# Merge gates in the tail: two more token quarters of four chunks in seven half-size products, with half of the sums of x on GpSimd

## The chip, the cores and the metric

The kernel runs on one core of a Trainium2 chip. A time is the device time of one execution in microseconds (us). A profile of one execution shows, for every instruction, when it started and how long it took on each engine: PE (TensorE, matrix products), DVE (VectorE), ACT (ScalarE), POOL (GpSimd) and SP (the queue that issues most DMAs). L1442 is line 1442 of the kernel; the change adds 5 lines ahead of almost everything and more further on, so the same statement has another number in the kernel after.

## The reference, cut to what matters

One layer of a hybrid attention block: `x` is 2048 tokens by 1024 channels, float32.

```python
h = rms_norm(x, norm_gain[layer])
proj = h @ w_in[layer]
qa, ka, va, qb, kb, vb, ga, gb, mg = jnp.split(proj, split_idx, axis=-1)
...                                     # two attention mixers give ya and yb
br_a = ya @ w_branch_a[layer]
br_b = yb @ w_branch_b[layer]
gates = jax.nn.sigmoid(mg.reshape(bsz, S, N_BRANCHES, D) + b_merge[layer])
merged = gates[:, :, 0] * br_a + gates[:, :, 1] * br_b
x = x + merged @ w_out[layer]
```

The change touches the product that gives `mg`, the merge-gate logits: 1024 channels of `h` times 2048 columns (1024 for each of the two branches), for 2048 tokens.

## The kernel before, in words

**Numbers.** Every float32 operand of a product is split into two float16 parts, a high one and a low one, and a product is the sum of three float16 products (high·high, high·low, low·high). The normalized `x`, transposed, lies in SBUF as `XH` and `XL` (128 partitions, 8 channel chunks, 2048 tokens and 256 tokens repeated).

**Stages.** A first stage loads and turns `x`; a long main loop projects and does both attentions; a tail follows. The tail has three stages: the merge gates, the branch products, the output product. The merge gates are cut by columns into chunks of 2 x 128 (one 128 for each branch), and by tokens into four quarters of 512. The first chunk is done in the main loop. The five others are numbered n = 0 to 4 here, in the order of use.

**Two ways for one chunk.** `gate_pair(n, q)` does one quarter plainly: 2 branches x 8 channel chunks x 3 = 48 matmuls of 128x512. `gate_group(n)` does quarters 0 and 2 together with Strassen's scheme in Winograd's form. The weights make a 2x2 of blocks (4 channel chunks by one branch), `x` another (4 channel chunks by one quarter); seven products of 12 matmuls take the place of eight. For that it needs sums: of the weight blocks (T1, T2, T3, N4; `w_sums`) and of the blocks of `x` (S1 to S4; `x_sums`). A sum of `x` is made in float32 from high plus low (the function `whole`), then split again: ACT rounds the high part (`hi`), DVE makes the low part (`lo`). The sums of `x` are the same for all chunks. In the kernel before, DVE makes all of them, in four groups c = 0 to 3 of one channel chunk each, into places of the buffer `wt` that is needed only later.

**Preparation of a chunk's weights** (`prep`): SP loads them into the one raw buffer `wraw` (four DMAs), POOL multiplies by the norm gains (four operations, L194), ACT squares and adds up (four, L236), PE adds across partitions in one small matmul (`norm_sum`, L211, whose input is `wsq`), DVE works out a power of two as scale, ACT and DVE split (L253, L259), and `w_sums` overwrites `wraw` with the sums of blocks (L1484) and splits these (L1485, L1481). The next chunk's load waits until `wraw` has been read for the last time.

**Output weights.** The last stage also uses seven-product groups; `b_load` and `b_blocks` bring in and split column parts j = 0 to 3 of `w_out` and their sums (L1340, L1341, L1362), in the gate stage.

**What sets the order.** The kernel is recorded with a list of events: `at(t, f)` puts a function at a planned time, and matmuls move the plan's clock (2.6 us for each 12). The tables `T_P`, `T_O`, `T_S` and so on hold such times. Only the order that comes out matters on the chip: each engine takes its instructions strictly in that order and waits where an input isn't there. So a late POOL operation holds up everything behind it on POOL, and a matmul that waits holds up every matmul behind it. In the plan before, PE does quarters 1 and 3 of n = 0 plainly, two of the seven products of n = 0, quarters 1 and 3 of n = 1, and so on: five groups of seven and ten plain quarters.

PSUM gives the tail eight banks of 128x512 (`bank`), used in turn.

Of the kernel before, what the change touches and what calls it, by code (L numbers as in the profile page):

```python
# [32 lines left out]
S = 2048  # L33
# [71 lines left out]
T_G = (143.4, 174.8, 176.0, 177.4)  # L105
T_S = (2.0, 11.0, 0.85, 1.6, 0.75, 1.5, 0.9, 1.3, 0.8)
# [18 lines left out]
def block_kernel(tc, x, w_units, w_gate, w_mrg, w_brn, w_out, w_bra, gain, qkg, sink, bias_a, bias_b, b_merge, out):  # L125
# [1073 lines left out]
    t = 0  # L1199
# [98 lines left out]

    rho, invb = {}, []
    bnd = ucol()  # L1300
    for k, (s, inv) in enumerate(((sa, ia), (sb, ib))):
        mi = ucol()
        V.tensor_tensor(mi[:], yi[4 * k][:], yi[4 * k + 1][:], OP.max)
# [11 lines left out]
    V.tensor_tensor(bnd[:], invb[0][:], invb[1][:], OP.add)
    V.tensor_scalar(bnd[:], bnd[:], 2.0 ** 31, None, OP.mult)
    s_m, i_m = pow2(bnd[:], "m")

    inv_m, rmx = ucol(), ucol()
    V.tensor_tensor(inv_m[:], invb[0][:], invb[1][:], OP.max)  # L1320
    V.reciprocal(rmx[:], inv_m[:])
    for c in range(8):
        V.tensor_scalar(rho[c][:], rho[c][:], invb[c // 4][:], rmx[:], OP.mult, OP.mult)
    V.tensor_scalar(inv_m[:], inv_m[:], s_m[:], 0.125, OP.mult, OP.mult)
    i_o, so4 = ucol(), ucol()
    V.tensor_scalar(i_o[:], i_m[:], io[:], 16.0, OP.mult, OP.mult)
    V.tensor_scalar(so4[:], so[:], 0.25, None, OP.mult)

# [64 lines left out]
    def gate_pair(n, q):  # L1393
        dc, u = DCS[n + 1], NU + 1 + n
        if n not in ims:
            assert ("w", u) in done
            ims[n] = ucol()
            V.tensor_scalar(ims[n][:], wtiles[u][2][:], 0.5 / SX, None, OP.mult)
        for k in range(2):
            ps = bank()  # L1400
            g = fg.tile([128, 512], F32, name="fg", bufs=6)
# [22 lines left out]

    def xsum(i, c):
        m = 4 * i + c
        return [wt[k][:, m % 7, 1 + m // 7, :] for k in range(2)]

    def xblock(b, c):
        if b in sidx:  # L1430
            assert ("xs", sidx[b], c) in done
            return xsum(sidx[b], c)
        o = 1024 if b == A22 else 0
        return [X[:, c + (0 if b == A11 else 4), o:o + 512] for X in (XH, XL)]

    def x_sums(t, c):

        tmp = y0.tile([128, 4, 512], F32, name=f"Y0{c % 2}")
        v1, v2, v3, v4 = (tmp[:, i, :] for i in range(4))

        def whole(o, ch, tok):
            V.tensor_tensor(o, XH[:, ch, tok:tok + 512], XL[:, ch, tok:tok + 512], OP.add)  # L1442

        def hi(v, i):
            A.activation(xsum(i, c)[0], v, AF.Copy, scale=0.25)

        def lo(v, i):
            h, l = xsum(i, c)
            V.scalar_tensor_tensor(l, v, 0.25, h, OP.mult, OP.subtract)
            done.add(("xs", i, c))  # L1450

        steps = ((whole, v1, c, 1024), (whole, v2, c + 4, 1024), (V.tensor_tensor, v2, v1, v2, OP.add), (hi, v2, 0),
                 (whole, v3, c, 0), (V.tensor_tensor, v1, v3, v1, OP.subtract), (lo, v2, 0), (hi, v1, 2),
                 (V.tensor_tensor, v3, v2, v3, OP.subtract), (hi, v3, 1), (whole, v4, c + 4, 0), (lo, v1, 2),
                 (V.tensor_tensor, v4, v4, v3, OP.subtract), (hi, v4, 3), (lo, v3, 1), (lo, v4, 3))
        for k, (f, *args) in enumerate(steps):
            at(t + T_S[2] * k, f, *args)

    tw = {}

    def w_sums(t, n):

        u = NU + 1 + n

        def begin():
            raw, s, inv, wh, wl = wtiles[u]
            q4 = ucol()
            V.tensor_scalar(q4[:], s[:], 0.25, None, OP.mult)
            t2 = [yq.tile([128, 512], F32, name="yq")[:].bitcast(F16).rearrange("p (b c d) -> p b c d", b=2, c=4) for _ in range(2)]
            b11, b12, b21, b22 = (raw[:, 4 * i:4 * i + 4, 128 * j:128 * j + 128] for i in range(2) for j in range(2))  # L1470
# [5 lines left out]
            for k, (b, o, x, y) in enumerate(((T1, o1, b12, b11), (T3, o3, b22, b12), (T2, o2, b22, o1), (N4, o4, b21, o2))):  # L1476
# [6 lines left out]

                at(now[0] + (T_S[3] if n else .72) * k, lambda o=o, x=x, y=y: V.tensor_tensor(o, x, y, OP.subtract))  # L1484
                at(now[0] + T_S[3] * k + T_S[4], lambda h=h, o=o, q4=q4: A.activation(h, o, AF.Copy, scale=q4[:]))  # L1485
# [3 lines left out]

    def gate_group(n):  # L1490
        dc, u = DCS[n + 1], NU + 1 + n
# [20 lines left out]
        def products(ps, x, bl):  # L1512
            mm = []
            for ch in range(4):
                for k, w in ((0, 0), (1, 0), (0, 1)):
                    i = len(mm)
                    mm.append(lambda ch=ch, k=k, w=w, i=i: T.matmul(  # L1517
                        ps[:], lhsT=weight(bl, ch)[w], rhs=xblock(x, ch)[k], start=(i == 0), stop=(i == 11)))
            return mm

        def copy(o, ps, scale):
            A.activation(o, whole(ps), AF.Copy, scale=scale)

        def plus(o, ps, v, scale):
            V.scalar_tensor_tensor(o, whole(ps), scale, v, OP.mult, OP.add)

# [3 lines left out]
        def gate(o, v, k, q, late):  # L1530
            at(now[0] + late, lambda: A.activation(o, v, AF.Tanh, bias=bmh[:, 8 * k + dc:8 * k + dc + 1], scale=ims[n][:]))
            at(now[0] + late + T_S[6], lambda: nc.sync.dma_start(out=whole(mgd[2 * dc + k][:, 512 * q:512 * q + 512]), in_=o))

# [10 lines left out]
        for k, (x, bl, f) in enumerate(steps):  # L1544
            if k == 0 and n:
                a = tile_()
# [5 lines left out]

    t = clock[0]
    for n, b, d in T_P:
        w_sums(t + d, n)
        if n:
            prep(t + b, NU + 1 + n)
    for c in range(4):
        at(t + T_S[0] + T_S[1] * c, x_sums, t + T_S[0] + T_S[1] * c, c)
    for j, b, d in T_O:  # L1560
# [18 lines left out]
    y_part(t + T_G[3], 0, 2, 0.9)  # L1579
    group0 = gate_group(0)  # L1580
    for n, q in ((0, 1), (0, 3), (group0, 2), (1, 1), (1, 3), (group0, 5), (gate_group(1), 7), (2, 1), (2, 3),
                 (gate_group(2), 7), (gate_group(3), 7), (gate_group(4), 7), (3, 1), (3, 3), (4, 1), (4, 3)):
        if isinstance(n, int):
            gate_pair(n, q)
        else:
            for _ in range(q):
                next(n)
    until(clock[0] + T_GATE[4] + .1)
    f1.close()
# [265 lines left out]
```

## Time and profile before

| what | value |
|---|---|
| median of 3 runs | 1910.09 us (1909.49 to 1910.53) |
| the profiled execution: span of its instructions | 1907.4 us |
| how the two stand | the median lies 2.7 us above the span |
| PE busy | 1898.5 us of the span |
| DVE, ACT, POOL busy | 1355.2, 1119.2, 848.7 us |
| gate stage of the tail | from 1399 us to 1593 us |
| branch stage | 1593 to 1759 us |
| output stage | 1759 us to the end |

In a timeline each row gives start, duration, engine, line, operation, output<-inputs, shape and count; a bracket gives the idle time of the engine before it and what ended it. In a table by stretches, each engine has its busy time and, in brackets, the number of its instructions. Names of tiles leave out buffer numbers: `wt` is the buffer of the sums of `x` and later of `w_out`, `fg` a gate tile, `Y` a temporary of 128x512, `yq` a small pool that also holds T2 and N4, `fps` and `pj` PSUM banks, `ubuf` a table of single columns (scales).

### The profile page before, as it was taken

The page shows a single profiled execution, that of the slowest core. Times are in us where ns is not written, and L with a number is a line of the kernel's source. Part 1 is how long each engine was busy: PE and PEld are TensorE (multiplying, and loading weights), DVE is VectorE, ACT ScalarE, POOL GpSimd, SP SyncE. Part 2 cuts the span into 40 slices and gives each one's busy share as a digit, 9 for nine tenths or more (in the row PEclk, how much of TensorE's full clock was granted, in tenths as well). Part 3 has the DMA queues.
Part 4 walks back from the last instruction along what each step waited for, and adds up shares of the span by engine and source line. Part 5 has one row for each costly group of instructions (what it writes and reads, how often), then busy time and mean ns, then how long its engine had stood idle before and what let it go on. Part 6 is the DMA issues. An engine that isn't in the chain of part 4 may idle for free.

```text
span 1907.4 us, 39286 instructions
## 1 busy us (share of the span) xinstructions
PE 1898.5 (100%) x13578; PEld 1190.9 (62%) x13578; DVE 1355.2 (71%) x3522; ACT 1119.2 (59%) x2496; POOL 848.7 (44%) x1848
## 2 busy tenths in 40 slices
PE   8999999999999999999999999999999999999999
PEld 6566776677766688566787667876544444444444
DVE  7578887887767877577776877868686667867312
ACT  8468776777666776566776767666444645423100
POOL 4334454344545655446555666555412211223443
PEclk9999999999999999999999999999999999999999
DMA  8459987798868697578768788666822246887853
GB/s 292 122 106 182 195 171 149 150 195 157 189 108 195 132 186 135 123 149 183 165 128 156 159 181 145 131 125 124 189 73 100 105 155 221 236 253 246 282 209 137
DMA packets 624585, 316.56 MB, mean 166 GB/s; under 512 B 492928, under 2 KB 562176, under 8 KB 623104
## 3 DMA queue, kind: packets, MB, share of 16 engines
q1 hardware_dynamic: 605952, 305.39, 69.3%
q10 hardware_dynamic: 18432, 8.66, 1.8%
q8 instruction: 106, 1.74, 0.4%
q14 instruction: 95, 0.78, 0.1%
HBM read 129.91 MB, written 65.27 MB: 102 GB/s over the span
## 4 chain that ended last, share of the span: by engine, by line
PE 95%; DVE 2%; POOL 1%; issue 1%; ACT 1%; DMA 0%; SPq 0%; DVEq 0%; POOLq 0%; ACTq 0%
PE pj L710 44%; PE pj L334 16%; PE fps L334 11%; PE fps L1722 6%; PE s L880 5%; PE pv L929 5%; PE fps L1517 3%; PE pj L1722 2%; PE pj L610 2%; PE pj L1517 1%; ACT jk L482 0%; DMA xt<-in_x_dram 0%; PE pt L1001 0%; DVE XL L531 0%; DVE pr L895 0%
## 5 line engine op out<-in xcount | busy, mean ns | idle before, releaser
L710 PE MATMUL pj<-wh,XL 128*128 128x384 f16 x1792 | 586.1, 327 | 0.0
L710 PE MATMUL pj<-wl,XH 128*128 128x384 f16 x1792 | 584.7, 326 | 0.0
L710 PE MATMUL pj<-wh,XH 128*128 128x384 f16 x1792 | 584.4, 326 | 0.2 <-DVE vt L742 0.2
L710 PEld LDWEIGHTS <-XH 128*128 128x128 f16 x3584 | 410.4, 116 | 151.0 <-issue 0.9
L895 DVE CUSTOM_DVE_ANT_0 pr<-s,b,ubuf 128x256 f32<-128x256 f32 (+3 forms) x512 | 219.0, 465 | 77.3 <-PE s L880 75.3
L710 PEld LDWEIGHTS <-XL 128*128 128x128 f16 x1792 | 207.8, 116 | 69.1
L912 DVE SCALAR_TENSOR_TENSOR p<-pr,p 128x512 f16<-128x512 f32 (+2 forms) x256 | 190.2, 743 | 19.1 <-ACT p L908 19.0
L787 POOL COPY spl<-spl 128x256 f16<-128x256 f16 (+1 forms) x224 | 88.6, 425 | 183.3 <-DVE spl L782 181.9
L727 ACT ACTIVATE rw<-pj 128x256 f32<-128x256 f32 (+1 forms) x224 | 86.8, 387 | 134.4 <-PE pj L710 123.2
L908 ACT ACTIVATE p<-pr 128x512 f16<-128x512 f32 (+2 forms) x256 | 159.2, 622 | 6.4 <-issue 0.3
L334 PEld LDWEIGHTS <-wh 128*128 128x128 f16 x960 | 93.7, 98 | 110.5
L880 PE MATMUL s<-kq 128*128 128x256 f16 (+3 forms) x1168 | 147.8, 254 | 0.3 <-DMA kq<-spl 0.3
L929 PEld LDWEIGHTS <-pt 128*128 128x128 f16 x3024 | 125.4, 97 | 34.8
L287 POOL TENSOR_TENSOR rs_t<-rs_y 128x8 f32<-128x8 f32 (+1 forms) x112 | 41.2, 368 | 231.3 <-DVE rs_y L279 182.7
L772 POOL TENSOR_TENSOR rw<-rw,g 128x256 f32<-128x256 f32 (+1 forms) x112 | 91.4, 816 | 109.5 <-DVE rw L766 73.1
L194 POOL TENSOR_TENSOR wraw<-wraw,gn 128x768 f32<-128x768 f32 (+1 forms) x80 | 112.5, 1412 | 56.0 <-DMA wraw<-in_w_mrg_dram 43.5
L929 PE MATMUL pv<-vt,pt 128*128 128x65 f16 (+1 forms) x3024 | 132.7, 192 | 0.0
L880 PEld LDWEIGHTS <-kq 128*128 128x128 f16 x1184 | 101.7, 98 | 42.3 <-DMA kq<-spl 0.8
L766 DVE TENSOR_TENSOR rw<-rw,qr 128x512 f32<-128x512 f32 (+1 forms) x112 | 102.6, 916 | 32.0 <-POOL qr L296 31.1
L742 DVE SCALAR_TENSOR_TENSOR vt<-pj,vt 128x128 f16<-128x128 f32 (+1 forms) x224 | 62.1, 277 | 88.6 <-ACT vt L736 87.9
L334 PE MATMUL pj<-XH,gh 128*128 128x512 f16 x320 | 121.3, 379 | 0.0
L334 PE MATMUL pj<-XH,gl 128*128 128x512 f16 x320 | 121.2, 379 | 0.0
(281 smaller groups left out, 3797.9 us busy)
## 6 DMA issues: line engine op xcount, KB each, us to landing
wraw<-in_w_units_dram SPq DMA_DIRECT2D x56, 384.0 KB, 4.4
mtd<-mm SPq DMA_DIRECT2D x56, 256.0 KB, 3.7
M<-mtd SPq DMA_DIRECT2D x8, 1792.0 KB, 9.8
mgd<-fg SPq DMA_DIRECT2D x39, 256.0 KB, 2.1
zd<-z ACTq DMA_DIRECT2D x128, 66.0 KB, 2.5
zz<-zd SPq DMA_DIRECT2D x64, 132.0 KB, 2.8
xt<-in_x_dram SPq DMA_DIRECT2D x16, 512.0 KB, 9.3
gtd<-yo SPq DMA_DIRECT2D x32, 256.0 KB, 2.9
```

The costliest lines, as they stand in the source:

```text
L194: G.tensor_tensor(v, v, gn[:, c0:c0 + 2].unsqueeze(2).to_broadcast([128, 2, n]), OP.mult)
L334: out.append(lambda w=w, xx=xx, ch=ch, i=i: T.matmul(ps[:], lhsT=w[:, ch, c0:c0 + 128], rhs=xx[:, ch, ts], start=(i == 0), stop=(i == n - 1)))
L710: out.append(lambda lhs=lhs, rhs=rhs, ch=ch, k=k: T.matmul(ps[:, :384], lhsT=lhs[:, ch, :], rhs=rhs[:, ch, :], start=(k == 0), stop=(k == ...
L766: V.tensor_tensor(q, q, self.rr[:, :n].unsqueeze(2).to_broadcast([128, n, HD]), OP.mult)
L772: G.tensor_tensor(k, k, GT[un.br][:].unsqueeze(1).unsqueeze(1).to_broadcast([128, 2, un.nk, HD]), OP.mult)
L787: G.tensor_copy(sp[:, i, nh:, :, :], sp[:, i, nq:nh, ::-1, :])
L880: T.matmul(self.sv[j][:, o:o + k1 - k0], lhsT=q[:, h, qo:qo + 128], rhs=kt[:, un.nq + kh + v * un.nk, k0:k1], start=(v == 0), stop=(v == 1))
L895: V.tensor_tensor_reduce(out=self.pv[:, j, self.p0:self.p0 + W], in0=self.sv[j], in1=un.bias[:, self.h0 + j, self.b0:self.b0 + W], scale=I ...
L908: A.activation(self.sp[:, :128 * n], self.pr, AF.Copy, scale=PSC)
L912: V.scalar_tensor_tensor(self.sp[:, 128 * n:], self.pr, PSC, self.sp[:, :128 * n], OP.mult, OP.subtract)
L929: T.matmul(self.po[:, j, :w], lhsT=p[:, n * j + s, :], rhs=un.v[key][:, vh, c0:c0 + w], start=(k == 0 and s == 0), stop=(k == 2 and s == n ...
L1722: mm.append(lambda ch=ch, k=k, w=w, i=i: T.matmul(ps[:, :cols.stop - cols.start], lhsT=m[:, a, ch, k, :], rhs=wt[w][:, b, ch, cols], start ...
```

## The change

Chunks n = 1 to 4 get a second group of seven products for quarters 1 and 3; chunk 0 keeps its two plain quarters. The sums of `x` are made a second time, for quarters 1 and 3 (called p = 1; S1 and S2 go to a new buffer `sx`, S3 and S4 over the part of `XH` and `XL` that has been used up). For c = 2 and 3 POOL makes the additions (`whole` and the others); `lo` stays on DVE, `hi` on ACT. The weight sums of n = 1 to 4 move from DVE to POOL too. T2 and N4 of n = 3 and 4 go to the repeated tokens of `XH` and `XL`. The scales for the later stages, worked out at the start of the tail in one run, become a generator that is stepped through at planned times from 60 us on. Part j = 3 of the output weights moves from the end of the gate stage into the branch stage. `prep` gets a shift that puts `norm_sum` and what follows later by 6.0, 7.0, 5.5 and 1.0 us for n = 1 to 4. A reserved scratch for DMA descriptors is set smaller; it is memory only.

```diff
-T_P = ((0, 0.0, 0.03), (1, 3.0, 50.0), (2, 56.0, 75.0), (3, 82.0, 102.0), (4, 108.5, 128.3))
-T_O = ((0, 62.0, 84.0), (1, 136.4, 154.0), (2, 136.9, 164.6), (3, 183.9, 190.0))
+T_P = ((0, 0.0, 0.03, 0.0), (1, 3.0, 30.6, 6.0), (2, 39.6, 67.4, 7.0), (3, 73.0, 99.5, 5.5), (4, 105.6, 127.5, 1.0))
+T_O = ((0, 62.0, 88.0), (1, 134.4, 147.2), (2, 134.9, 155.4))
+T_OB = (58.0, 66.0)
+T_X = {(0, 0): (0.6, 0.85), (0, 1): (10.2, 0.85), (0, 2): (0.3, 1.35), (0, 3): (11.9, 1.35),
+       (1, 0): (23.0, 0.95), (1, 1): (33.0, 1.1), (1, 2): (24.0, 1.8), (1, 3): (39.5, 1.9)}
...
+    sx = fin.enter_context(tc.tile_pool(name="sx", bufs=1)).tile([128, 8, 2, 512], F16, name="sx")
...
-    def x_sums(t, c):
-
-        tmp = y0.tile([128, 4, 512], F32, name=f"Y0{c % 2}")
-        v1, v2, v3, v4 = (tmp[:, i, :] for i in range(4))
+    def x_sums(t, c, p, d):
+        E = V if c < 2 else G
+
+        if c < 2:
+            tmp = y0.tile([128, 4, 512], F32, name=f"Y0{c}")
+            v1, v2, v3, v4 = (tmp[:, i, :] for i in range(4))
+        else:
+            v1, v2, v3, v4 = (wt[k][:, 5 + i, 2 - i:4 - i, :].rearrange("p a b -> p (a b)").bitcast(F32)
+                              for k in range(2) for i in range(2))
...
-            V.tensor_tensor(o, XH[:, ch, tok:tok + 512], XL[:, ch, tok:tok + 512], OP.add)
+            tok += 512 * p
+            E.tensor_tensor(o, XH[:, ch, tok:tok + 512], XL[:, ch, tok:tok + 512], OP.add)
...
-                at(now[0] + (T_S[3] if n else .72) * k, lambda o=o, x=x, y=y: V.tensor_tensor(o, x, y, OP.subtract))
+                at(now[0] + (T_S[3] if n else .72) * k, lambda o=o, x=x, y=y: (G if n else V).tensor_tensor(o, x, y, OP.subtract))
...
-    for n, q in ((0, 1), (0, 3), (group0, 2), (1, 1), (1, 3), (group0, 5), (gate_group(1), 7), (2, 1), (2, 3),
-                 (gate_group(2), 7), (gate_group(3), 7), (gate_group(4), 7), (3, 1), (3, 3), (4, 1), (4, 3)):
+    for q in (1, 3):
+        gate_pair(0, q)
+    for n, p in ((0, 0), (1, 0), (1, 1), (2, 0), (2, 1), (3, 0), (4, 0), (3, 1), (4, 1)):
+        for _ in gate_group(n, p):
+            pass
...
+    at(t + T_OB[0], b_load, 3)
+    at(t + T_OB[1], b_blocks, t + T_OB[1], 3)
```

How the order of instructions changes, at three places. First POOL at the start of the tail, before; the last operations of the main loop (`zz`), then the gains of chunks n = 1 and 2 (`wraw`) and the additions of the gate groups (L1528).

```order
L1112 TENSOR_TENSOR zz<-zz,bm_e 128x4x64 x3
L194 TENSOR_TENSOR wraw<-wraw,gn 128x2x256 x4
L1528 TENSOR_TENSOR wt_21862<-fg 128x2x256
L1528 TENSOR_TENSOR fg<-fg 128x512
L194 TENSOR_TENSOR wraw<-wraw,gn 128x2x256 x4
```

POOL at the same place in the kernel after, up to the gains of n = 1; `wt_21866` and `wt_21867` are the two halves of `wt`, here the temporaries of c = 2.

```order
L1117 TENSOR_TENSOR zz<-zz,bm_e 128x4x64 x3
L1466 TENSOR_TENSOR wt_21866<-XH,XL 128x512 x2
L439 TENSOR_TENSOR wt_21866<-wt_21866 128x512
L1466 TENSOR_TENSOR wt_21867<-XH,XL 128x512
L439 TENSOR_TENSOR wt_21866<-wt_21867,wt_21866 128x512
L439 TENSOR_TENSOR wt_21867<-wt_21866,wt_21867 128x512
L1466 TENSOR_TENSOR wt_21867<-XH,XL 128x512
L199 TENSOR_TENSOR wraw<-wraw,gn 128x2x256 x2
L439 TENSOR_TENSOR wt_21867<-wt_21867 128x512
L199 TENSOR_TENSOR wraw<-wraw,gn 128x2x256 x2
```

The sums of c = 2 now stand ahead of and between the gains of n = 1, those of c = 3 behind them. Further on in the same queue, the gains of n = 2 among the sums of c = 3 for p = 1:

```order
L439 TENSOR_TENSOR wt_21866<-wt_21866 128x512
L199 TENSOR_TENSOR wraw<-wraw,gn 128x2x256
L1466 TENSOR_TENSOR wt_21867<-XH,XL 128x512
L199 TENSOR_TENSOR wraw<-wraw,gn 128x2x256
L439 TENSOR_TENSOR wt_21866<-wt_21867,wt_21866 128x512
L199 TENSOR_TENSOR wraw<-wraw,gn 128x2x256 x2
L439 TENSOR_TENSOR wt_21867<-wt_21866,wt_21867 128x512
```

From the first sum to the last of these gains stand 43 POOL operations: 8 gains and 35 of two full operands (sums, weight sums, two additions of a gate group). In the kernel before 10 stood there.

Second, PE in the kernel after, where the small matmul of n = 2 (`norm_sum`, L216) now is: in the group of n = 1, p = 1, right ahead of its product with S1 (`sx`); 288 matmuls of 128x512 stand ahead of it in the gate stage.

```order
L1547 MATMUL fps<-XL,wh 128x512
L1547 LDWEIGHTS wl
L1547 MATMUL fps<-XH,wl 128x512
L216 LDWEIGHTS ones
L216 MATMUL pj<-wsq,ones 128x4
L1547 LDWEIGHTS wh
L1547 MATMUL fps<-sx,wh 128x512
```

Before, it stood behind 331 matmuls, and DVE, not POOL, had made all sums. Third, DVE at the start of the tail in the kernel after (`Y_21886` holds weight sums of n = 0, `Y_21891` the sums of c = 0); before, 40 operations on single columns (the scales, L1303 to L1327) stood between the first row here and the second.

```order
L231 RECIPROCAL ubuf<-ubuf 128x1
L1412 TENSOR_SCALAR ubuf<-ubuf 128x1
L1499 TENSOR_SCALAR ubuf<-ubuf 128x1
L1519 TENSOR_TENSOR Y_21886<-wraw 128x512
L1466 TENSOR_TENSOR Y_21891<-XH,XL 128x512
L1519 TENSOR_TENSOR Y_21886<-wraw 128x512
```

DVE begins its sums that much sooner, and makes 80 operations with two SBUF operands (64 for the sums of `x`, 12 for weight sums, 4 for the split of n = 1) up to the last low part of the sums for p = 1.

More of the change, by code (lines that the diff above doesn't have):

```diff
@@ L1315, in block_kernel @@
[L1315 to L1325, printed above, removed]
@@ L1326, in block_kernel, with tail_scales, tt @@
-    V.tensor_scalar(i_o[:], i_m[:], io[:], 16.0, OP.mult, OP.mult)
-    V.tensor_scalar(so4[:], so[:], 0.25, None, OP.mult)
+    rho, invb = [ucol() for _ in range(8)], []
+    bnd, inv_m, rmx, i_o, so4 = (ucol() for _ in range(5))
+    def tail_scales():
+        def tt(*a):
+            V.tensor_tensor(*(v[:] for v in a[:-1]), a[-1])
+        V.tensor_scalar(so4[:], so[:], 0.25, None, OP.mult)
+        for k, (s, inv) in enumerate(((sa, ia), (sb, ib))):
+            mi, rm, iv = ucol(), ucol(), ucol()
+            for c in range(3):
+                tt(mi, mi if c else yi[4 * k], yi[4 * k + c + 1], OP.max)
+                yield
+            V.reciprocal(rm[:], mi[:])
+            yield
+            tt(rm, rm, s, OP.mult)
+            tt(iv, mi, inv, OP.mult)
+            yield
+            for c in range(4 * k, 4 * k + 4):
+                tt(rho[c], rm, yi[c], OP.mult)
+            invb.append(iv)
+        tt(bnd, invb[0], invb[1], OP.add)
+        tt(inv_m, invb[0], invb[1], OP.max)
+        yield
+        V.tensor_scalar(bnd[:], bnd[:], 2.0 ** 31, None, OP.mult)
+        V.reciprocal(rmx[:], inv_m[:])
+        yield
+        s_m, i_m = pow2(bnd[:], "m")
+        for c in range(8):
+            V.tensor_scalar(rho[c][:], rho[c][:], invb[c // 4][:], rmx[:], OP.mult, OP.mult)
+        V.tensor_scalar(inv_m[:], inv_m[:], s_m[:], 0.125, OP.mult, OP.mult)
+        V.tensor_scalar(i_o[:], i_m[:], io[:], 16.0, OP.mult, OP.mult)
@@ L1334, in block_kernel, with run @@
+    def run(steps):
+        if next(steps, run) is not run:
+            at(now[0] + T_R[1], run, steps)
     A11, A12, A22, S1, S2, S3, S4 = range(7)
@@ L1400, in gate_pair @@
             ps = bank()
[L1401 removed]
+            g = fg.tile([128, 512], F32, name="fg", bufs=7)
             def tanh(ps=ps, g=g, k=k):
@@ L1418, in prep, with xsum, xblock @@
         chain(sq)
     sidx = {S1: 0, S2: 1, S3: 2, S4: 3}
[L1425 to L1429, printed above, removed]
+    def xsum(p, i, c):
+        if p == 0:
+            m = 4 * i + c
+            return [wt[k][:, m // 3, 1 + m % 3, :] for k in range(2)]
+        if i < 2:
+            return [sx[:, 4 * i + c, k, :] for k in range(2)]
+        return [X[:, c, 512 * i:512 * i + 512] for X in (XH, XL)]
+    def xblock(b, c, p):
@@ L1465, in begin @@
         def begin():
+            assert ("w", u) in done, (n, now[0] - t0)
             raw, s, inv, wh, wl = wtiles[u]
@@ L1531, in gate @@
             at(now[0] + late, lambda: A.activation(o, v, AF.Tanh, bias=bmh[:, 8 * k + dc:8 * k + dc + 1], scale=ims[n][:]))
-            at(now[0] + late + T_S[6], lambda: nc.sync.dma_start(out=whole(mgd[2 * dc + k][:, 512 * q:512 * q + 512]), in_=o))
+            at(now[0] + late + T_S[6], lambda: nc.sync.dma_start(out=mgd[2 * dc + k][:, 512 * (q + p):512 * (q + p) + 512], in_=o))
         def two(ps):
@@ L1544, in gate_group @@
         for k, (x, bl, f) in enumerate(steps):
-            if k == 0 and n:
+            if k == 0:
                 a = tile_()
@@ L1551, in gate_group @@
             yield
-    t = clock[0]
-    for n, b, d in T_P:
+    t = t0 = clock[0]
+    at(t + T_R[0], run, tail_scales())
+    for n, b, d, late in T_P:
         w_sums(t + d, n)
         if n:
-            prep(t + b, NU + 1 + n)
+            prep(t + b, NU + 1 + n, late)
     for c in range(4):
-        at(t + T_S[0] + T_S[1] * c, x_sums, t + T_S[0] + T_S[1] * c, c)
+        for p in range(2):
+            b, d = T_X[p, c]
+            at(t + b, x_sums, t + b, c, p, d)
     for j, b, d in T_O:
@@ L1579, in block_kernel @@
     y_part(t + T_G[3], 0, 2, 0.9)
-    group0 = gate_group(0)
-    for n, q in ((0, 1), (0, 3), (group0, 2), (1, 1), (1, 3), (group0, 5), (gate_group(1), 7), (2, 1), (2, 3),
-                 (gate_group(2), 7), (gate_group(3), 7), (gate_group(4), 7), (3, 1), (3, 3), (4, 1), (4, 3)):
[L1583 to L1588, printed above, removed]
+    for q in (1, 3):
[3 more added lines that the diff above has]
+            pass
+    until(clock[0] + T_GATE[0] + T_S[8] + T_S[6] + .05)
     f1.close()
```

81 lines of the change are left out of this document (37 added, 44 removed).

## Prediction

> **What bounds the kernel now.** I read the table of engines and the row of granted clocks first, then the chain of waits, then busy time by stretch in the tail.
>
> ```profile
> span 1907.4 us, 39286 instructions
> PE 1898.5 (100%) x13578; PEld 1190.9 (62%) x13578; DVE 1355.2 (71%) x3522; ACT 1119.2 (59%) x2496; POOL 848.7 (44%) x1848
> PEclk9999999999999999999999999999999999999999
> PE 95%; DVE 2%; POOL 1%; issue 1%; ACT 1%; DMA 0%; SPq 0%; DVEq 0%; POOLq 0%; ACTq 0%
> core 0: us, PE busy (x) PEld busy (x) DVE busy (x) ACT busy (x) POOL busy (x), PEclk, DMA share, GB/s
> 1399.00:1590.00 191.00, 190.97 (x889) 86.63 (x888) 131.23 (x223) 100.81 (x169) 33.32 (x26) 1.00 0.36 120
> 1399.00:1471.00 72.00, 71.97 (x336) 32.62 (x335) 54.85 (x99) 35.48 (x62) 13.97 (x11) 1.00 0.27 95
> 1400.00:1443.50 43.50, 43.47 (x204) 19.65 (x202) 42.98 (x78) 23.54 (x41) 5.38 (x4) 1.00 0.22 79
> ```
>
> PE is the bound, at full clock, and in the gate stage it stands still for 0.03 us in all. So a matmul taken out is worth its whole pitch, and any wait put in costs its whole length. The last two rows show where room is short: in the first 43.5 us DVE is as full as PE, because it makes the sums of `x` there, and POOL is nearly empty.
>
> **Matmuls removed.** Four groups of seven take the place of eight plain quarters: four times 12 matmuls fewer, 48. Between the second and the first stretch lie 889 - 336 = 553 matmuls in 119.0 us of PE, 0.215 us each; 48 x 0.215 = **-10.3 us**. This is certain as far as PE has its inputs.
>
> **Sums added.** DVE and POOL together make the sums twice. What an operation costs depends on its neighbour:
>
> ```profile
> 1407.13 0.68 DVE L1442 TENSOR_TENSOR Y<-XH,XL 128x512 f32<-128x512 f16 x1
> ...
> 1409.96 1.52 DVE L1449 SCALAR_TENSOR_TENSOR wt<-Y,wt 128x512 f16<-128x512 f32 x1
> 1411.41 1.52 DVE L434 TENSOR_TENSOR Y<-Y 128x512 f32<-128x512 f32 x1
> 1412.85 1.52 DVE L1442 TENSOR_TENSOR Y<-XH,XL 128x512 f32<-128x512 f16 x1
> 1414.30 0.68 DVE L1449 SCALAR_TENSOR_TENSOR wt<-Y,wt 128x512 f16<-128x512 f32 x1
> 1414.90 0.68 DVE L434 TENSOR_TENSOR Y<-Y 128x512 f32<-128x512 f32 x1
> 1415.50 1.28 DVE L1442 TENSOR_TENSOR Y<-XH,XL 128x512 f32<-128x512 f16 x2
> ```
>
> ```profile
> 1408.45 5.38 POOL L194 TENSOR_TENSOR wraw<-wraw,gn 128x512 f32<-128x512 f32 x4 [24.66 <-DMA wraw<-in_w_mrg_dram]
> 1451.89 1.76 POOL L1528 TENSOR_TENSOR wt<-fg 128x512 f32<-128x512 f32 x1 [38.06 <-ACT wh L1485]
> 1472.57 1.71 POOL L1528 TENSOR_TENSOR fg<-fg 128x512 f32<-128x512 f32 x1 [1.36 <-DVE fg L1525]
> 1510.63 1.26 POOL L1528 TENSOR_TENSOR fg<-fg 128x512 f32<-128x512 f32 x1 [16.91 <-issue]
> 1513.92 4.04 POOL L194 TENSOR_TENSOR wraw<-wraw,gn 128x512 f32<-128x512 f32 x4
> ```
>
> With POOL idle, DVE starts such an operation every 0.60 us (1414.30, 1414.90, 1415.50). While POOL multiplies gains (1408.45 to 1413.83), DVE's starts lie 1.45 apart (1409.96, 1411.41, 1412.85), and POOL's four take 5.38 us, not 4.04. The two take turns: a gain lengthens DVE's sequence by 1.45 - 0.60 = 0.85 us. A full addition on POOL takes 1.26 us alone (L1528) and 1.71 to 1.76 beside DVE, so I take 1.70 for a pair and **1.1 us** (1.70 - 0.60) for what it adds to DVE's sequence. Thus work given to POOL is not work taken away: an addition that took DVE 0.60 us takes the pair 1.1.
>
> Now the sequence, from DVE's first operation of the tail:
>
> ```profile
> 1394.74 0.17 DVE L226 RECIPROCAL ubuf<-ubuf 128x1 f32<-128x1 f32 x1
> 1394.82 0.14 DVE L1303 TENSOR_TENSOR ubuf<-ubuf 128x1 f32<-128x1 f32 x1
> ...
> 1400.75 0.14 DVE L1327 TENSOR_SCALAR ubuf<-ubuf 128x1 f32<-128x1 f32 x1
> ```
>
> The scales that go elsewhere fill 1394.82 to 1400.89, so DVE begins its sums at 1394.9, 6 us sooner; put in singly later, the same 40 small operations cost about the same 6 us (1.3 of it before the point below, where 8 of them stand). POOL can begin sooner still: its temporaries lie in memory that PE's last transposes free.
>
> ```profile
> 1387.95 0.60 PE L1001 MATMUL pt<-idf,ya 128*128 128x128 f32 x4
> 1398.77 0.38 PE L334 MATMUL fps<-XH,wh 128*128 128x512 f16 x1
> ```
>
> From 1388.5 to 1394.9 POOL makes 6.4 / 1.27 = 5 of its 35 additions alone. Up to the last gain of chunk n = 2, 30 additions and 8 gains are left: 30 x 1.1 + 8 x 0.85 = 39.8 us. In DVE's queue stand 78 of its 80 two-operand operations ahead of that point (POOL's sums for one c wait for DVE's low parts of the sums before, whose temporaries they overwrite, so POOL can't run ahead): 78 x 0.60 = 46.8. Six evacuations of PSUM at 0.60 and the 1.3 add 4.9. Sum 91.5, and 1394.9 + 91.5 = **1486.4**. ACT squares that gain:
>
> ```profile
> 1416.15 0.61 ACT L236 ACTIVATE wl<-wraw 128x512 f16<-128x512 f32 x1
> 1416.67 0.19 ACT L236 ACTIVATION_READ_ACCUMULATOR wl<-wraw 128x1 f32 x1
> ```
>
> That gives 1487.2, when the small matmul `norm_sum` of n = 2 has its input. In the new order of PE it stands behind 288 matmuls of the stage, and PE gets there at 1398.77 + 288 x 0.215 = 1460.8. PE waits **26.4 us**, and with it everything queued behind: the product with S1, and all others. Smaller waits ahead of it (the first sums of p = 0) don't add, since this one ends at a fixed time. The sums for p = 1, wanted right behind, are ready at about that time too.
>
> Bounds: if every POOL operation cost only the 0.85 of a gain, the 30 additions take 7.5 us less, and PE waits 18.9. If the POOL additions of two float16 operands, which no row shows, are dearer, or DVE or POOL waits on the other's results now and then, I allow 10 us more: 36.
>
> **Weight sums moved to POOL.** For each of n = 1 to 4 these are four operations; on DVE they took 0.77 us:
>
> ```profile
> L1525 DVE SCALAR_TENSOR_TENSOR fg<-fps,fg 128x512 f32<-128x512 f32 x16 | 11.0, 689 | 24.2 <-PE fps L1517 17.1 <-ACT wl L236 4.2 <-POOL fg L1528 1.4
> L1484 DVE TENSOR_TENSOR wraw<-wraw 128x512 f32<-128x512 f32 x12 | 9.2, 768 | 0.0
> ```
>
> On POOL, 1.27 to 1.71: 2 to 4 us later per chunk, and as much later for the one raw buffer and the next load. Chunks n = 3 and 4 can each wait once more for this; 0 to 10 us, and I take **5**, as part of it lies behind PE's lateness already.
>
> **Part j = 3 moved.** Seven roundings on ACT, seven splits and four subtractions on DVE go to about 1658 us.
>
> ```profile
> 1640.00:1660.00 20.00, 20.00 (x95) 9.01 (x93) 16.82 (x27) 8.00 (x16) 4.59 (x3) 1.00 0.70 203
> 1660.00:1680.00 20.00, 20.00 (x94) 9.11 (x93) 13.60 (x21) 6.76 (x11) 6.71 (x5) 1.00 0.95 284
> L1341 DVE SCALAR_TENSOR_TENSOR wt<-wraw,ubuf,wt 128x512 f16<-128x512 f32 x7 | 5.1, 747 | 0.7 <-ACT wt L1340 0.5
> L1362 DVE TENSOR_TENSOR wraw<-wraw 128x512 f32<-128x512 f32 x4 | 2.7, 687 | 0.0
> ```
>
> 7.8 us of DVE (5.1 + 2.7) meet 3.2 + 6.4 = 9.6 free in these 40 us, behind eight PSUM banks of 12 x 0.215 = 2.6 us each. Cost 0; without that cover up to 2. The added roundings of sums on ACT (16 more) fit in its free 90 us of the gate stage: 0. The seventh gate tile and the smaller scratch issue nothing.
>
> **Sum.** -10.3 + 26.4 + 5 = +21.1 us on the span of 1907.4. The median of the runs, 1910.09, lies 2.7 above that span, and I add the change to it: **1931 us**. Its own range: late 18.9 and nothing later gives 1919; late 36 and 10 later gives 1946.
>
> **Rivals.** A, *the engines overlap freely*. By averages there is room: POOL is busy 33.32 of 191 us, DVE 131.23. DVE alone needs 51.7 us, to 1446.6, and POOL's 43 operations alone would end at 1388.5 + 35 x 1.27 + 8 x 1.04 = 1441.3, both before 1460.8. Then only the matmuls count: 1910.1 - 10.3 = 1899.8. Against it stand the starts 1.45 apart. Chance 0.14.
>
> B, *POOL's own pace decides*: each POOL operation takes one turn beside one of DVE's and never waits for DVE. 30 x 1.70 + 8 x 1.35 = 61.8 from 1394.9: 1456.7, still ahead of PE. What is left is the 5 us of the later chunks: 1904.8. For it, POOL's 1.70 already holds a turn of DVE; against it, POOL's temporaries wait for the low parts, and DVE has 40 more operations than POOL. Chance 0.08.
>
> C, *the long waits cost more than their length*. PE's idle times in this trace are short, as this one of 0.97 us in the first stage:
>
> ```profile
> 23.40 0.28 PE L610 MATMUL pj<-XH,gl 128*128 128x256 f16 x1 [0.97 <-DVE gl L387]
> ```
>
> No row shows what a wait of 10 or 26 us does. If sums and weights come in pieces, each wait gives some matmuls at half pace, and the late evacuations push the later chunks to the far end of their 10 us: 1931 + 5 and some more, 1936 to 1942, and I write 1938. Chance 0.16. The Trainium skill, "TensorE: Matmul & The Clock Gate", section "Part 1: The HAM clock gate", says that PE's clock drops to half after an idle window of some 3.4 us and comes back after as long a time of work. By that rule each wait of over 3.4 us would cost an estimated 1.7 us on top, and two or three such waits 3 to 5, which would give 1935 or so; no run here shows it so far.
>
> **How the numbers follow.** The forecast, with its own range of 1919 to 1946, has 0.62; A 0.14, B 0.08, C 0.16. A run of this kernel can tell about 0.2% (3.8 us) from no change. Faster by more than that: A, B (0.22). Within it: a forecast whose wait is just 10 us (0.03, out of the 0.62). Slower: the rest, 0.75. For 8 in 10 the range reaches down to B and up over C's middle: 1904 to 1943, which leaves out A and the far end.
>
> **What would show it.** Right: in the gate stage after, POOL's additions of `x` take about 1.7 us and DVE's sums 1.3 to 1.5; PE's idle time lies mostly before 1490, at `norm_sum` of n = 2 and the products with sums, and ends with ACT's square or DVE's low part; the stage lasts 16 us longer, not 10 shorter. A is right if those durations stay at 1.27 and 0.68 and PE is never idle. B is right if they are long but the last gain of n = 2 ends before 1461. C shows matmuls at more than 0.215 us behind a wait, or a granted clock under 1.00. I am wrong on the later chunks if PE is idle for more than 10 us after 1500, and on part j = 3 if it is idle between 1650 and 1690.

## The result, and the profile after

The changed kernel takes 1943.12 us (median of 4 runs, 1942.41 to 1943.25), the kernel before in the same sessions 1910.31: a ratio of 1.0173, with an interval of 1.0159 to 1.0188. It is 32.8 us slower. The forecast was 1931, and 1943.12 lies just above the upper end of the stated range, 1943.

The page after, with its table of engines and the row of granted clocks:

```profile
span 1941.2 us, 39310 instructions
PE 1901.7 (98%) x13530; PEld 1187.6 (61%) x13530; DVE 1404.0 (72%) x3542; ACT 1131.5 (58%) x2520; POOL 936.9 (48%) x1904
PEclk9999999999999999999999999999998999999999
```

PE has 48 matmuls fewer, as the change says, and is no longer busy all the time. Where the time went is best seen by counting matmuls in stretches of the same length. Three stretches of the tail (the first part of the gate stage, its later part, the branch stage), of the kernel before:

```profile
1400.00:1490.00 90.00, 89.97 (x420) 40.77 (x418) 70.20 (x122) 47.45 (x81) 17.62 (x14) 1.00 0.28 99
1500.00:1565.00 65.00, 65.00 (x303) 29.48 (x302) 36.95 (x61) 31.89 (x52) 11.98 (x10) 1.00 0.44 146
1600.00:1740.00 140.00, 140.00 (x650) 63.50 (x649) 108.97 (x159) 50.77 (x81) 35.62 (x25) 1.00 0.82 256
```

The same lengths at the same places of the kernel after (the branch stage begins later there):

```profile
1400.00:1490.00 90.00, 72.11 (x297) 29.78 (x295) 85.92 (x92) 39.84 (x73) 62.14 (x39) 0.89 0.15 53
1500.00:1565.00 65.00, 58.34 (x263) 25.75 (x262) 44.97 (x99) 34.78 (x61) 33.05 (x26) 0.97 0.27 95
1620.00:1760.00 140.00, 134.68 (x619) 60.20 (x617) 103.84 (x152) 52.60 (x84) 34.29 (x24) 1.00 0.77 241
```

At 0.215 us for a matmul, 420 - 297 = 123 matmuls fewer are 26.4 us lost, 303 - 263 = 40 are 8.6 us, and 650 - 619 = 31 are 6.7 us: 41.7 us. With -10.3 for the matmuls removed this gives +31.4, and the span grew by 33.8. The other 2.4 us are lost outside these stretches, 1.5 of them ahead of 1400: PE begins the gate stage at 1400.30, not at 1398.77. In the first stretch PE is idle for 17.9 us (90.00 - 72.11) and the granted clock is 0.89, so the rest of the 26.4, some 8.5 us, lies in slower matmuls.

What PE waited for in the tail after (us in total, times, longest):

```profile
PE pj L216 <- ACT wl L241: 8.0, 3, 4.7
PE pj L1547 <- DVE yq L1516: 6.9, 2, 5.9
PE pj L1547 <- ACT wh L1520: 2.7, 1, 2.7
PE fps L339 <- DVE kp L1688: 2.3, 2, 2.1
PE pj L1547 <- ACT wt L1469: 2.0, 1, 2.0
```

L216 is `norm_sum`, L1547 a product of a group of seven, L339 one of the branch stage. DVE and POOL between 1388 and 1490 us, grouped by line (L1466 and L439 are the additions for the sums of `x`, L1519 those for the weights):

```profile
L1466 POOL TENSOR_TENSOR wt<-XH,XL 128x512 f32<-128x512 f16 x16 | 24.5, 1538 | 11.9 <-DVE wt L1472 7.0 <-PE pt L1006 4.8
L1466 DVE TENSOR_TENSOR Y<-XH,XL 128x512 f32<-128x512 f16 x16 | 19.7, 1239 | 0.0
L439 DVE TENSOR_TENSOR Y<-Y 128x512 f32<-128x512 f32 x16 | 18.4, 1153 | 0.1
L439 POOL TENSOR_TENSOR wt<-wt,wt 128x512 f32<-128x512 f32 x8 | 13.1, 1638 | 0.3
L1519 POOL TENSOR_TENSOR wraw<-wraw 128x512 f32<-128x512 f32 x4 | 8.0, 2011 | 5.4 <-DVE wl L264 5.4
```

The same addition takes DVE 1.15 to 1.24 us on the mean, not 0.68, and POOL 1.54 to 1.64. The first gain of n = 2, the addition behind its last gain, the last low part of `sx`, and `norm_sum` of n = 2:

```profile
1476.62 1.07 POOL L199 TENSOR_TENSOR wraw<-wraw,gn 128x512 f32<-128x512 f32 x1 [2.24 <-DMA wraw<-in_w_mrg_dram]
1485.23 1.72 POOL L439 TENSOR_TENSOR wt<-wt,wt 128x512 f32<-128x512 f32 x1
1488.20 0.69 DVE L1472 SCALAR_TENSOR_TENSOR sx<-wt,sx 128x512 f16<-128x512 f32 x1
1488.83 0.16 PE L216 MATMUL pj<-wsq,ones 128*128 128x4 bf16 x1 [2.11 <-ACT wl L241]
```

The last gain ended when the addition behind it began, at 1485.2; the forecast had it at 1486.4, and `norm_sum` at 1487.2, where it ran at 1488.8. PE idles only 2.1 us at this place, since it had been held up before, above all at the weight sums of n = 1. None of PE's waits is for a sum of p = 1, but the sums were no sooner: the last low part of `sx`, which the two products behind `norm_sum` read, ended at 1488.9. The longest wait:

```profile
1468.52 4.45 PE L1547 MATMUL pj<-wt,yq 128*128 128x512 f16 x10 [5.95 <-DVE yq L1516]
```

This row shows the clock too: the ten matmuls behind the 5.95 us of waiting take 4.45 us, some 0.43 us apart, twice the usual.

### The profile page after: what moved, and what is told of

It reads as the page before. It is cut to its first block, busy times and chain, and to the rows that moved or that the text cites. A ratio compares the mean times of both kernels' runs of the same rounds, so it can differ in the third digit from the quotient of the medians.

```text
span 1941.2 us, 39310 instructions
## 1 busy us (share of the span) xinstructions
PE 1901.7 (98%) x13530; PEld 1187.6 (61%) x13530; DVE 1404.0 (72%) x3542; ACT 1131.5 (58%) x2520; POOL 936.9 (48%) x1904
## 5 line engine op out<-in xcount | busy, mean ns | idle before, releaser
L747 DVE SCALAR_TENSOR_TENSOR vt<-pj,vt 128x128 f16<-128x128 f32 (+1 forms) x224 | 62.1, 277 | 89.4 <-ACT vt L741 88.8
L339 PEld LDWEIGHTS <-wh 128*128 128x128 f16 x704 | 68.5, 98 | 86.6 <-issue 5.6
L339 PE MATMUL pj<-XH,gh 128*128 128x512 f16 x320 | 121.3, 379 | 0.0
L339 PE MATMUL pj<-XH,gl 128*128 128x512 f16 x320 | 121.2, 379 | 0.0
```

The lines of the kernel that those rows point to most:

```text
L339: out.append(lambda w=w, xx=xx, ch=ch, i=i: T.matmul(ps[:], lhsT=w[:, ch, c0:c0 + 128], rhs=xx[:, ch, ts], start=(i == 0), stop=(i == n - 1)))
```

## The experiments

**1. Who makes the sums of `x`.** All of them on DVE:

```diff
-        E = V if c < 2 else G
+        E = V
```

> The changed kernel with all sums of x on DVE; the weight sums stay on POOL. Theory (DVE and POOL take turns): an addition on POOL beside DVE adds about 1.0 us to DVE's sequence and on DVE 0.60, so about 26 additions moved back save 26 x 0.4 = 10 us, of which the 5 to 6 that POOL had made before DVE began give 3 back: norm_sum of n = 2 some 6 to 7 us sooner than 1488.8, time 1935 to 1938 against 1943.1, and DVE's sums take 0.68 us, not 1.2. Rival (POOL relieves DVE): DVE gets 31 operations of 0.6 us more, norm_sum up to 15 us later, time 1950 to 1960.

Measured: 1937.56 us, 5.6 less than the changed kernel (ratio to before 1.0145, 1.0130 to 1.0160). DVE's groups between 1394.9 and 1490 us:

```profile
L1466 DVE TENSOR_TENSOR wt<-XH,XL 128x512 f32<-128x512 f16 x16 | 12.8, 801 | 0.0
L1466 DVE TENSOR_TENSOR Y<-XH,XL 128x512 f32<-128x512 f16 x16 | 12.7, 801 | 0.0
L439 DVE TENSOR_TENSOR Y<-Y 128x512 f32<-128x512 f32 x16 | 12.6, 788 | 0.0
```

DVE has 32 additions more and is done sooner (`norm_sum` of n = 2 runs at 1483.35, not at 1488.83): one that DVE makes takes 0.80 us, not 1.24 beside POOL. Turns, not relief. What is left over 0.68 is due to POOL's gains, weight sums and group additions, which still fall among them.

**2. Who makes the weight sums.**

```diff
-                at(now[0] + (T_S[3] if n else .72) * k, lambda o=o, x=x, y=y: (G if n else V).tensor_tensor(o, x, y, OP.subtract))
+                at(now[0] + (T_S[3] if n else .72) * k, lambda o=o, x=x, y=y: V.tensor_tensor(o, x, y, OP.subtract))
```

> The changed kernel with the weight sums of n = 1 to 4 back on DVE; half of the sums of x stay on POOL. Theory: they are 4 additions per chunk, each 1.0 on POOL against 0.6 on DVE, so 2 us for n = 1 and less for the others: 1940 to 1942. Rival (the chain of weight sums on POOL is itself what PE waits for, 5.9 us at the second T2/N4 part of n = 1 and 2 to 5 us more for n = 2 to 4): 1933 to 1936.

Measured: 1940.43 us (1.0159, 1.0144 to 1.0174), 2.7 less than the changed kernel, as the theory has it. The two intervals overlap, but in the trace too `norm_sum` of n = 2 runs 2.7 us sooner, at 1486.09. The wait at T2 and N4 of n = 1 fell from 5.9 to 2.7 us, and `norm_sum` of n = 2 took part of it over (4.4 us, not 2.1; the 5.6 below is that of n = 4). Rows of its waits:

```profile
PE pj L216 <- ACT wl L241: 11.3, 3, 5.6
PE pj L1547 <- DVE yq L1516: 2.7, 1, 2.7
```

So the weight sums were the last thing awaited there, and not what made it late.

**3. Both.** The two edits together.

> Both: all sums of x and all weight sums on DVE, POOL only the gains and the additions of the gate groups. Theory: the two savings add up, 1932 to 1936; PE still waits some 25 us in all, since DVE alone has 80 operations to make before PE wants the last of them. Rival (without POOL's share DVE is the longer one): over 1943.

Measured: 1934.88 us (1.0132, 1.0117 to 1.0147): 8.2 less than the changed kernel, where the parts gave 5.6 and 2.7. They add up. `norm_sum` of n = 2 runs at 1481.86, 7.0 us sooner. So the additions that POOL was given cost 8 of the 43 us lost (32.8, and the 10.3 that the matmuls bring); the rest stays with POOL nearly out of it and has another cause.

**4. The second set of sums left out.** The groups for p = 1 use the sums of p = 0.

```diff
-        for p in range(2):
+        for p in range(1):
             b, d = T_X[p, c]
...
-            assert ("xs", p, sidx[b], c) in done
-            return xsum(p, sidx[b], c)
+            return xsum(0, sidx[b], c)
```

> The changed kernel without the second set of sums (p = 1 is computed with the sums of p = 0, so the gates of quarters 1 and 3 of n = 1 to 4 are those of other tokens): the matmuls, weight sums, order of the rest and the moved part j = 3 stay. Theory (the second set of sums doesn't fit ahead of where PE wants it): PE's waits before 1490 fall from 27 to about 6 us, those of n = 2 and 4 after it to 0 to 5, the 7 us in the branch stage stay: 1910.3 - 10.3 + 6 + 2 + 7 = 1915, 1908 to 1919. Rival (the weights' chains on POOL and DVE cost it): over 1925.

Measured: 1914.36 us (1.0022, 1.0012 to 1.0031). The two stretches of the gate stage:

```profile
1400.00:1490.00 90.00, 86.35 (x394) 38.60 (x393) 68.97 (x125) 42.98 (x75) 44.76 (x32) 0.98 0.26 86
1500.00:1565.00 65.00, 63.78 (x297) 28.74 (x296) 41.23 (x70) 36.83 (x61) 24.48 (x18) 1.00 0.40 137
```

PE makes 394 matmuls where it made 297, and 297 where it made 263; DVE is busy 69 of 90 us, not 86. The second set of sums, which doesn't fit ahead of where PE wants it, costs 28.8 us; all other parts of the change together lose what the 48 matmuls bring and 4 us more. Among these, the shift in `prep` and the scales made at other times were not tried alone. The loads of `wraw` show how the lateness goes on. Chunks n = 1 to 4 here:

```profile
1403.44 1.93 SPq L194 DMA_DIRECT2D wraw<-in_w_mrg_dram  x4
1454.06 3.97 SPq L194 DMA_DIRECT2D wraw<-in_w_mrg_dram  x4
1486.30 1.93 SPq L194 DMA_DIRECT2D wraw<-in_w_mrg_dram  x4
1519.95 1.92 SPq L194 DMA_DIRECT2D wraw<-in_w_mrg_dram  x4
```

And in the changed kernel:

```profile
1403.39 1.93 SPq L194 DMA_DIRECT2D wraw<-in_w_mrg_dram  x4
1473.28 1.92 SPq L194 DMA_DIRECT2D wraw<-in_w_mrg_dram  x4
1514.03 1.92 SPq L194 DMA_DIRECT2D wraw<-in_w_mrg_dram  x4
1547.68 1.92 SPq L194 DMA_DIRECT2D wraw<-in_w_mrg_dram  x4
```

Each load waits until the one raw buffer is free. In the changed kernel that of n = 2 comes 19 us later than here, and those of n = 3 and 4 come 28 us later, 33.7 us apart in both kernels; why the lateness grows behind n = 2 was not taken apart. PE spends only one group of 84 matmuls (18 us) between the beginnings of n = 3 and n = 4, half of what it spends on n = 2, so there the late chain is met: the 4.7 us wait of `norm_sum` at 1556, which is 0.4 us in this run.

**5. The branch stage: part j = 3 later.** The forecast put its move at 0, and the branch stage lost 6.7 us. First the part 42 to 44 us later in that stage, then (run 7) in the kernel before, then (8) back where it was.

```diff
-T_OB = (58.0, 66.0)
+T_OB = (100.0, 110.0)
```

> The changed kernel with part j = 3 of the output weights 42 to 44 us later in the branch stage (planned at 100 and 110 us of the stage, not at 58 and 66), where DVE has more room. Theory (the 4.9 us that PE waits between 1680 and 1740 in the changed kernel are these 11 DVE operations in a stretch where DVE is full): the waits there go, and few come behind: 1938 to 1940 against 1943.1. Rival (the waits come from DVE's other work, which is as late in this kernel as everything): 1942 to 1944.

Measured: 1944.38 us (1.0178, 1.0161 to 1.0195), no gain. The rival's number, but its reason isn't shown by this: the waits did move with the part, to 1752 to 1777.

**6. Turn-taking alone, in the kernel before.** Its additions for c = 2 and 3 go to POOL, nothing else.

```diff
+        E = V if c < 2 else G
...
-            V.tensor_tensor(o, XH[:, ch, tok:tok + 512], XL[:, ch, tok:tok + 512], OP.add)
+            E.tensor_tensor(o, XH[:, ch, tok:tok + 512], XL[:, ch, tok:tok + 512], OP.add)
```

> The kernel before, with nothing changed but the additions of c = 2 and 3, which POOL makes (16 additions; no second set, no other order). Theory (turns): 16 additions at 1.0 in place of 0.6 make the sequence of DVE and POOL 6 us longer in a stretch where DVE has no room: PE waits 2 to 5 us, 1912 to 1915 against 1910.1. Rival (POOL relieves DVE): no wait, 1910.

Measured: 1913.92 us (1.0022, 1.0013 to 1.0032). Half of the additions taken from DVE makes this kernel 4.3 us slower (the kernel before took 1909.59 in these sessions). What PE waited for in its gate stage is a low part that DVE makes too late:

```profile
PE pj L334 <- DVE wl L259: 3.6, 2, 1.9
```

**7. Part j = 3 moved, alone, in the kernel before.**

```diff
-T_O = ((0, 62.0, 84.0), (1, 136.4, 154.0), (2, 136.9, 164.6), (3, 183.9, 190.0))
+T_O = ((0, 62.0, 84.0), (1, 136.4, 154.0), (2, 136.9, 164.6))
...
+    at(t + T_OB[0], b_load, 3)
+    at(t + T_OB[1], b_blocks, t + T_OB[1], 3)
```

> The kernel before, with nothing changed but part j = 3, which goes from the end of the gate stage to 58 and 66 us of the branch stage, as in the changed kernel. Theory (DVE has no room there): PE waits 3 to 5 us in the branch stage, 1913 to 1915. Rival (the forecast: banks and DVE's free time hide it): 1910 to 1911.

Measured: 1910.26 us (1.0003, 0.9994 to 1.0012). My theory falls, and the forecast's 0 holds here: 650 matmuls in 140 us of the branch stage, as before.

**8. Part j = 3 back at the end of the gate stage, in the changed kernel.**

```diff
-T_O = ((0, 62.0, 88.0), (1, 134.4, 147.2), (2, 134.9, 155.4))
+T_O = ((0, 62.0, 88.0), (1, 134.4, 147.2), (2, 134.9, 155.4), (3, 174.6, 180.7))
...
-    at(t + T_OB[0], b_load, 3)
-    at(t + T_OB[1], b_blocks, t + T_OB[1], 3)
```

> The changed kernel with part j = 3 back at the end of the gate stage, 9 us sooner than before, as the planned stage is shorter. If the move alone cost the 5 us: 1938 to 1939. Rival (the stage now ends with groups of seven, whose evacuations need DVE, where the plain quarters before needed only ACT, so there is no room for j = 3 there either, and the y parts behind it are late): 1943 to 1948.

Measured: 1943.66 us (1.0177, 1.0162 to 1.0192), as the rival said. Now PE waits for the parts of `y` at the start of the branch stage:

```profile
PE fps L339 <- DVE Y L1292: 4.3, 5, 1.5
PE pj L339 <- DVE Y L1292: 1.8, 3, 0.9
```

So the move costs nothing in the kernel before, and in the changed one the time is lost wherever the part stands. Something else had used up the room. It shows at the start of the stage: PE's first product and DVE's first use of one, in the kernel before,

```profile
1593.31 0.59 PE L334 MATMUL fps<-Y,wh 128*128 128x512 f16 x2
1600.04 0.69 DVE L1658 SCALAR_TENSOR_TENSOR kp<-kp,fps 128x512 f32<-128x512 f32 x1 [1.05 <-DMA kp<-mgd]
```

and in the kernel after, with the stores of the last gates and the first load behind them on SP's queue:

```profile
1619.88 0.59 PE L339 MATMUL pj<-Y,wh 128*128 128x512 f16 x2
1625.24 1.73 SPq L1562 DMA_DIRECT2D mgd<-fg  x3
1627.06 0.41 SPq L1678 DMA_DIRECT2D kp<-mgd  x1
1630.31 0.69 DVE L1688 SCALAR_TENSOR_TENSOR kp<-kp,pj 128x512 f32<-128x512 f32 x1 [5.21 <-DMA kp<-mgd]
```

DVE began 6.7 us behind PE in the kernel before (4.5 in run 7), and 10.4 after: the stage now ends on a group of seven, whose last gates pass DVE, POOL and ACT before they are stored, and the first gate of the branch stage is loaded behind them. Eight PSUM banks hold 20.6 us of PE's work (8 x 12 x 0.215); the late start and the 7.8 us of part j = 3 on DVE draw on the same reserve. Run 4 lies in between: it has the part and the group of seven, and DVE starts 7.8 us behind PE and 21 matmuls are lost against 650 (4.5 us):

```profile
1593.52 0.59 PE L339 MATMUL pj<-Y,wh 128*128 128x512 f16 x2
1601.32 0.69 DVE L1687 SCALAR_TENSOR_TENSOR kp<-kp,pj 128x512 f32<-128x512 f32 x1 [5.31 <-DMA kp<-mgd]
1600.00:1740.00 140.00, 136.16 (x629) 61.19 (x628) 105.13 (x154) 49.42 (x79) 34.92 (x24) 1.00 0.81 251
```

The next two runs take one of the two away each.

**9. No part j = 3 at all.**

```diff
-    at(t + T_OB[0], b_load, 3)
-    at(t + T_OB[1], b_blocks, t + T_OB[1], 3)
...
-                    ps[:, :cols.stop - cols.start], lhsT=m[:, a, ch, k, :], rhs=wt[w][:, b, ch, cols], start=(i == 0), stop=(i == 11)))
+                    ps[:, :cols.stop - cols.start], lhsT=m[:, a, ch, k, :], rhs=wt[w][:, b, min(ch, 2), cols], start=(i == 0), stop=(i == 11)))
```

> The changed kernel without part j = 3 of the output weights at all (neither its load nor its 18 operations; the output product takes the blocks of j = 2 in its place, so a quarter of its terms are wrong). x7 showed that the move costs nothing in the kernel before. Theory (the branch stage starts 4 us late on DVE, as the first gate can be loaded only behind the last seven-product group's stores, and j = 3 takes the room that would make up for it: two delays, each hidden alone): without j = 3 the waits between 1680 and 1740 go and those at 1640 (1.7 us) stay, 1938 to 1939. Rival (DVE is late in the branch stage for another reason): 1942 to 1944.

Measured: 1938.61 us (1.0151, 1.0134 to 1.0168).

**10. The last group as two plain quarters.**

```diff
-    for n, p in ((0, 0), (1, 0), (1, 1), (2, 0), (2, 1), (3, 0), (4, 0), (3, 1), (4, 1)):
+    for n, p in ((0, 0), (1, 0), (1, 1), (2, 0), (2, 1), (3, 0), (4, 0), (3, 1)):
         for _ in gate_group(n, p):
             pass
+    for q in (1, 3):
+        gate_pair(4, q)
```

> The changed kernel with the last group of seven (n = 4, quarters 1 and 3) done as two plain quarters: 12 matmuls more, 2.6 us, and nothing but ACT needed behind the last of them (quarter 3 reads the part of XH that S4 has overwritten, so its gates are wrong). Theory (the late start of DVE in the branch stage is one of the two causes): DVE's first product of the branch stage comes 7 us behind PE's start, not 10.4, and the 6.8 us of waits there fall to 2 or less: 1943.1 + 2.6 - 5 = 1941, 1939 to 1942. Rival (the start plays no part): 1945 to 1946.

Measured: 1940.66 us (1.0165, 1.0150 to 1.0180), 2.5 less with 12 matmuls more. The start of its branch stage:

```profile
1623.25 0.59 PE L339 MATMUL fps<-Y,wh 128*128 128x512 f16 x2
1627.78 0.69 DVE L1690 SCALAR_TENSOR_TENSOR kp<-kp,fps 128x512 f32<-128x512 f32 x1 [4.59 <-DMA kp<-mgd]
```

DVE is 4.5 us behind PE. The matmuls of 140 us of the branch stage in runs 9 and 10:

```profile
1620.00:1760.00 140.00, 137.92 (x637) 62.12 (x636) 99.46 (x147) 49.66 (x79) 36.05 (x25) 1.00 0.77 243
```

```profile
1624.00:1764.00 140.00, 138.87 (x644) 62.66 (x642) 105.05 (x153) 50.92 (x82) 33.42 (x23) 1.00 0.81 249
```

Without part j = 3, 13 matmuls are lost against 650 (2.8 us); without the late start, 6 (1.3 us); with both, 31 (6.7 us). Each alone costs little, and both together more than their sum. This rests on the traces: the intervals of runs 9 and 10 overlap with that of the changed kernel, whose time they lower by 4.5 and 2.5 us. None of the runs is faster than the kernel before. Run 7, which is that kernel with the part moved, is as fast; of the runs of the changed kernel the nearest is run 4, 0.2% slower.

## Why the prediction was right or wrong, point by point

- **Matmuls removed, -10.3 us.** Right: 48 fewer, and the sum above closes only with them.
- **Turns between DVE and POOL.** Right, shown by runs 1, 3 and 6. The price was near: 1.1 us was taken for what an addition on POOL adds to the sequence, and POOL's additions took 1.54 to 1.64 us with a turn of DVE's 0.60 in them, so 0.95 to 1.0. The Trainium skill, "SBUF — State Buffer", section "SBUF: two separate sides", says that a DVE operation with two SBUF inputs and a GpSimd operation that reads SBUF lock each other out for a whole instruction; the trace agrees nearly: alone, 0.60 and 1.04 us make 1.64, and in turns the pair took 1.45. Rival A, that the two overlap freely, is out.
- **PE late by 26.4 us up to `norm_sum` of n = 2.** The size is right (123 matmuls, 26.4 us up to 1490), and the moment too (1487.2 against 1488.8). That they agree so closely is in part luck. The 30 additions and 8 gains on POOL took an estimated 36 us of DVE's time (88.8 us from 1396.43 to 1485.2, less 83 operations of its own at 0.60 us, its small ones and its waits), where 39.8 were forecast; DVE's sums began 1.5 us later than forecast (1396.43), and DVE waited 1.8 us in between. PE too began the stage 1.5 us later. The place was wrong: I had the wait at `norm_sum`, and only 2.1 us of it fell there. Smaller waits came before, at the first sums (2.0 us) and above all at the weights and weight sums of n = 1 (2.7 and 5.9). As the forecast said, they don't add to it, since the last one ends at a time that DVE sets: from 1396.43 to 1485.2 DVE is idle for 1.8 us only.
- **What makes it late.** Here the emphasis was wrong rather than a number. My working spent most words on the price of POOL's turns; runs 3 and 4 price them (with the weight sums) at 8.2 us and the second set of sums as a whole at 28.8. With every sum on DVE the kernel is still 1.3% slower. The forecast also had no wait for the raw buffer: the load of n = 2 began at 1473.28, behind the last split of n = 1's weight sums on DVE, and POOL waited 2.24 us for it.
- **Later chunks, 5 us (0 to 10).** Measured 8.6, inside the bound. The reason I gave, weight sums on POOL, is shown wrong for the larger part: in runs 2 and 3, with these on DVE, the longest wait of `norm_sum`, that of n = 4, is still 5.6 us. In run 4, without the lateness at n = 2, it is 0.4 us: that lateness arrives there through the one raw buffer.
- **Part j = 3 moved, 0 us, up to 2 without the cover of eight banks.** This is the step that failed, the largest of the terms that were too small; with the later chunks and the edges it put the time at the end of the range. As a move alone it costs 0, as worked out (run 7). In the changed kernel the branch stage lost 6.7 us, as DVE starts it 4 us later behind a group of seven, and the cover that I had named was spent twice (runs 9 and 10). The forecast has no term for a stage that ends on a group of seven, and it priced part j = 3 with the whole cover. The sign that I had named, PE idle between 1650 and 1690, did not come (0.24 us): in a stage that begins 26.6 us later the waits behind the part lie between 1713 and 1736. The upper bound of 2 came from DVE's average room in 40 us and didn't ask how late DVE already was when the stretch began.
- **Rival B, POOL's own pace,** is out: POOL's gain of n = 2 came at 1485, not at 1457, and its additions waited 7.0 us for DVE's low parts.
- **Rival C, waits that cost more than their length,** is in part right. The clock is below 1.00 in both stretches of the gate stage. The Trainium skill, "TensorE: Matmul & The Clock Gate", section "Part 1: The HAM clock gate", has the clock at half after an idle window of some 3.4 us, for about as long; the trace agrees on the half (0.43 us against 0.215 behind the wait of 5.95 us), and there it lasts longer, 5.9 us and 14 matmuls (a granted clock of 0.50 from 1468.5 to 1474.4). Where a later wait ends at a time that DVE sets, as up to 1488, the slow matmuls should cost nothing extra, as they fall in time that PE would have waited; no run takes them away to show it. Behind the wait at 1556 they cost 1.5 us (seven matmuls), which is in the 8.6.

The sum against the forecast: -10.3 for the matmuls (forecast -10.3), 26.4 (26.4), 8.6 (5), 6.7 (0) and 2.4 at the edges (0), together the 33.8 us by which the span grew.

## What to carry to other kernels

Before work is moved to an idle engine, look in the trace for the two engines side by side: here an addition handed from DVE to POOL cost the pair more than DVE alone, whatever the shares of busy time said. Compare the moment at which the last of the new inputs can be ready with the moment at which the bound engine wants it; fewer matmuls bring nothing where their inputs come 26 us late. When two edits are each priced at nothing because the same buffers hide them, price them together, and run them together.

## What the runs showed of the hardware that was not expected

PE's clock fell without a long wait. Two waits of 2.05 and 0.37 us close together at 1431.75, with one of 1.22 us 5 us before them, went with a granted clock of 0.83 in the ten microseconds from 1430, while one of 2.11 us that ended at 1488.83 left it at 1.00 in the ten from 1490. The first two waits in PE's timeline:

```profile
1431.75 0.38 PE L1547 MATMUL pj<-wt,wh 128*128 128x512 f16 x1 [2.05 <-ACT wt L1469]
1432.50 0.38 PE L1547 MATMUL pj<-wt,wh 128*128 128x512 f16 x1 [0.37 <-DVE wt L1472]
```

And the two stretches, with the granted clock in the third column from the end:

```profile
1430.00:1440.00 10.00, 7.88 (x28) 3.15 (x28) 9.30 (x12) 5.56 (x10) 4.21 (x3) 0.83 0.14 52
1490.00:1500.00 10.00, 10.00 (x48) 4.51 (x46) 5.35 (x18) 5.73 (x9) 3.58 (x4) 1.00 0.39 130
```

What decides between the two was not tried.
